# Two-layer hybrid block on one core: lookahead of three chunks in the mixer, the norm's gain on the activations, compression chunks spread through the weight stream

## The chip, the cores and the metric

One core of a Trainium2 chip runs the whole program. The metric is the device time of one execution in microseconds; three executions of the kernel before took 1166.40, 1166.65 and 1167.07 us, and the median, 1166.65 us, is what the change is measured against.

## What is computed

Two layers, each of a SwiGLU, a mixer and a second SwiGLU on 256 tokens of width 1024, each behind an RMS norm with a gain and added to the residual:

```python
for l in range(DEPTH):
    x = x + 0.5 * swiglu(rms_norm(x, norm_ffn1[l]), ffn1_wi[l], ffn1_wo[l])
    h = rms_norm(x, norm_mix[l])
    (u, q_raw, k_cmp, v_cmp, k_sel, v_sel, k_win, v_win,
     nsa_gate, gate_a, gate_b) = jnp.split(h @ w_in[l], SPLIT_POINTS, axis=-1)
    y_a = s5_branch(u, ...)                  # complex diagonal state space, 64 states for each of 32 groups
    y_b = nsa_branch(q_raw, k_cmp, ...) @ nsa_w_up[l]   # attention over compressed, selected and near keys
    merged = jax.nn.sigmoid(gate_a) * y_a + jax.nn.sigmoid(gate_b) * y_b
    x = x + merged @ w_out[l]
    x = x + 0.5 * swiglu(rms_norm(x, norm_ffn2[l]), ffn2_wi[l], ffn2_wo[l])
```

Compression takes the keys and values in blocks of 32 tokens through a 2048x128 matrix (`cmp_w1`), a GELU and a 128x64 matrix, once for keys and once for values.

## The kernel before

**Precision.** Each weight and each activation is split into a high part in fp32r (`whi`, `hh`) and the rest (`wlo`, `hl`), and a product is three matmuls, `mm3`: high by high (L381), high by low (L382), low by high (L383). ScalarE writes the high part and VectorE subtracts it for the low part. Weights arrive as chunks of 128x1024 (`raw`, 512 KB, four buffers) by DMA from SP's queue, in the order that `plan` writes down, and are split by `_split0`: a chunk with a norm's gain in pieces of one row block, with the gain multiplied in (L169 on ScalarE, L170 on VectorE), others in one piece (L349). `next` hands out a chunk and prepares `LA`=2 chunks ahead; there are four `whi` and four `wlo` buffers. Chunks of the compression (`cmp_w1`) are used unsplit, straight from `raw`, and hold a raw buffer until their products are done.

**Order.** A gemm (`gemm`) takes 256 tokens as two halves t0 and t1, each with a PSUM bank `gu` of which there are two, and runs `mm3` for each chunk of weights, t0 and t1 in turn. The bank is emptied by ScalarE (an evacuation), and the next gemm's first matmul of that half waits for it. Behind each chunk a background generator (`pull`) puts in a few steps of the state space branch (`s5_main`) and later of the attention. The framework fixes each engine's order when it builds the program; each engine then runs its instructions in that order, and a semaphore holds an instruction until its inputs and its buffer are there.

**The mixer** (`mix`) runs eight gemms over `w_in`, four chunks each: u (512 columns), KC (384), VS (408), Q (512), GA (2 x 512), GB (2 x 512). After u come the norm's sum of squares (`norms`, L363, tied behind the high part of the newest split), its evacuation (L1282) and a transposition on VectorE; then KC. After VS come the compression's four chunks with 16 products each (L550), and the small matrices; then Q, whose evacuation is L1049. GA and GB are evacuated by a tanh (L1322). The state space branch multiplies u into the state (L550), rotates (`rotate`, L933 to L941 on VectorE), scans (L890), rotates back, and then forms y from three products for each group, one of u and two of the rotated state (L907). The end of the SwiGLU ahead (`finish`) transposes the residual in pieces of 128x512 (L375) and splits them into `hh` and `hl` (L349).

## Time and profile before

| | |
|---|---|
| median of 3 executions | 1166.65 us |
| profiled execution | 1167.36 us |
| its span, first to last instruction | 1165.6 us |
| TensorE busy | 1153.3 us (99%) |
| VectorE busy | 827.1 us (71%) |
| ScalarE busy | 671.9 us (58%) |
| mean granted clock of TensorE | 0.997 |
| layer 0's mixer in the span | about 202 to 396 us |
| layer 1's mixer | about 780 to 972 us |

TensorE is the engine to look at: the others matter where it waits for them. Busy time of TensorE includes time at a lower clock, so the waits and the granted clock are read together.

### The profile page before, as it was taken

How to read it: one execution, taken by the hardware profiler on the slowest of the kernel's cores; microseconds unless marked ns; L12 is line 12 of the kernel's file. 1: busy time of each engine (PE TensorE's matmuls, PEld its weight loads, DVE VectorE, ACT ScalarE, POOL GpSimd, SP SyncE). 2: the span in 40 equal slices, each digit the busy share in tenths (PEclk: the TensorE clock that was granted, in tenths of full speed). 3: DMA queues.
4: the chain of work that ended last, by engine and by line, in shares of the span. 5: the costliest groups of instructions: out<-in, count | busy, mean ns of one | idle time of the engine just before them, and what ended most of it. 6: DMA issues, size and time to landing. Idle time of an engine off the chain costs nothing.

```text
span 1165.6 us, 17595 instructions
## 1 busy us (share of the span) xinstructions
PE 1153.3 (99%) x6148; PEld 939.7 (81%) x6148; DVE 827.1 (71%) x1578; ACT 671.9 (58%) x1176; POOL 96.0 (8%) x177
## 2 busy tenths in 40 slices
PE   9999999999999999999999999999999999999998
PEld 6888887877877888888888888788788778888886
DVE  5798597797776665555567986977987666655654
ACT  6755665646674565555566565555667646555552
POOL 3000000021032000000030000002112200000000
PEclk9999999999999999999999999999999999999999
DMA  8765646464443566665665555565654335766662
GB/s 239 232 193 166 186 144 209 124 204 141 155 118 106 174 206 191 187 183 185 192 181 184 181 179 169 157 178 158 200 162 145 109 110 170 227 184 185 191 183 88
DMA packets 150266, 200.40 MB, mean 172 GB/s; under 512 B 10145, under 2 KB 121025, under 8 KB 150177
## 3 DMA queue, kind: packets, MB, share of 16 engines
q1 hardware_dynamic: 148656, 196.93, 55.4%
q0 software_dynamic: 1136, 1.82, 0.8%
q8 instruction: 48, 0.79, 0.3%
q10 hardware_dynamic: 384, 0.52, 0.2%
q14 instruction: 42, 0.34, 0.1%
HBM read 198.18 MB, written 1.05 MB: 171 GB/s over the span
## 4 chain that ended last, share of the span: by engine, by line
PE 95%; DVE 3%; ACT 1%; issue 0%; POOL 0%; DVEq 0%; ACTq 0%; POOLq 0%
PE gu L381 20%; PE gu L383 20%; PE gu L382 20%; PE yb L382 4%; PE yb L383 4%; PE yb L381 4%; PE ya L383 4%; PE ya L381 4%; PE ya L382 4%; PE tr L496 2%; PE yb L1238 1%; PE yb L907 1%; PE tr L375 1%; PE tr L1227 1%; PE gu L448 1%; PE ya L1194 1%
## 5 line engine op out<-in xcount | busy, mean ns | idle before, releaser
L169 ACT ACTIVATE whi<-raw,gcol 128x512 fp32r<-128x512 f32 (+2 forms) x480 | 316.2, 710 | 197.8 <-PE gu L382 84.7
L170 DVE SCALAR_TENSOR_TENSOR wlo<-raw,gcol,whi 128x512 fp32r<-128x512 f32 (+2 forms) x480 | 335.6, 738 | 108.2 <-ACT whi L169 106.2
L381 PE MATMUL gu<-whi,hh 128*128 128x512 f32 (+2 forms) x944 | 373.5, 396 | 1.8 <-ACT r L1322 1.8
L383 PE MATMUL gu<-wlo,hh 128*128 128x512 f32 (+2 forms) x944 | 367.7, 393 | 0.0
L382 PE MATMUL gu<-whi,hl 128*128 128x512 f32 (+2 forms) x944 | 367.6, 389 | 0.0
L349 DVE TENSOR_TENSOR wlo<-raw,whi 128x1024 fp32r<-128x1024 f32 x128 | 156.5, 1225 | 120.0 <-ACT whi L349 117.2
L381 PEld LDWEIGHTS gu<-whi,hh 128*128 128x128 f32 x944 | 177.9, 188 | 36.3 <-ACT r L1322 2.6
L382 PEld LDWEIGHTS gu<-whi,hl 128*128 128x128 f32 x944 | 178.1, 189 | 34.8 <-issue 0.2
L383 PEld LDWEIGHTS gu<-wlo,hh 128*128 128x128 f32 x944 | 177.3, 188 | 34.8 <-issue 0.3
L349 ACT CAST whi<-raw 128x1024 fp32r<-128x1024 f32 x128 | 134.4, 1053 | 121.2 <-PE gu L382 102.4
L382 PE MATMUL yb<-whi,w1k 128*128 128x512 f32 x176 | 71.2, 406 | 0.2
L382 PE MATMUL ya<-whi,w1k 128*128 128x512 f32 x176 | 68.7, 392 | 0.0
L383 PE MATMUL yb<-wlo,w1k 128*128 128x512 f32 x176 | 68.1, 392 | 0.0
L381 PE MATMUL yb<-whi,w1k 128*128 128x512 f32 x176 | 68.0, 393 | 0.0
L381 PE MATMUL ya<-whi,w1k 128*128 128x512 f32 x176 | 67.6, 394 | 0.0
L383 PE MATMUL ya<-wlo,w1k 128*128 128x512 f32 x176 | 67.1, 390 | 0.0
L349 ACT CAST w1k<-tr 128x256 fp32r<-128x256 f32 x88 | 32.4, 368 | 43.5 <-PE tr L496 43.1
L513 DVE SCALAR_TENSOR_TENSOR w1k<-gu,rs,w1k 128x256 f32<-128x256 f32 x88 | 42.0, 479 | 16.8 <-ACT w1k L512 16.8
L512 ACT ACTIVATE w1k<-gu,rs 128x256 f32<-128x256 f32 x88 | 40.9, 467 | 18.4 <-PE gu L383 15.7
L356 POOL TENSOR_SCALAR rs<-ss 128x1 f32<-128x1 f32 (+3 forms) x22 | 6.8, 309 | 523.8 <-ACT w2k L363 472.3
L1217 POOL TENSOR_SCALAR w2k<-w2k,sm 128x128 f32<-128x128 f32 (+1 forms) x64 | 35.1, 568 | 103.8 <-DVE sm L1209 48.6
L349 DVE TENSOR_TENSOR w1k<-tr,w1k 128x256 fp32r<-128x256 f32 x88 | 36.6, 419 | 9.9 <-ACT w1k L349 9.8
(316 smaller groups left out, 1378.9 us busy)
## 6 DMA issues: line engine op xcount, KB each, us to landing
raw<-in_ffn_wi_dram SPq DMA_DIRECT2D x352, 256.0 KB, 3.3
raw<-in_ffn_wo_dram SPq DMA_DIRECT2D x88, 512.0 KB, 3.6
raw<-in_w_in_dram SPq DMA_DIRECT2D x48, 512.0 KB, 4.5
raw<-in_ssm_w_glu_dram SPq DMA_DIRECT2D x32, 256.0 KB, 3.0
raw<-in_w_out_dram SPq DMA_DIRECT2D x16, 512.0 KB, 3.7
raw<-in_cmp_w_dram SPq DMA_DIRECT2D x8, 512.0 KB, 4.9
raw<-in_nsa_w_up_dram SPq DMA_DIRECT2D x16, 256.0 KB, 4.0
raw<-in_w_in_dram SPq DMA_DIRECT2D x8, 408.0 KB, 4.2
```

Source lines behind the costliest of these rows:

```text
L169: k.hi_ins[i] = k.nc.scalar.activation(hi[:, s], r[:, s], AF.Copy, scale=c)
L170: k.lo_ins = k.nc.vector.scalar_tensor_tensor(lo[:, s], r[:, s], c, hi[:, s].bitcast(F32), op0=ALU.mult, op1=ALU.subtract)
L349: return k.nc.scalar.copy(hi, src), k.nc.vector.tensor_sub(lo, src, hi.bitcast(F32))
L375: m = k.nc.tensor.transpose(b[:, i], src[:, i * 128:(i + 1) * 128], k.id)
L381: mm(ps, a[0], b[0], start=first, stop=False)
L382: mm(ps, a[1], b[0], start=False, stop=False)
L383: return mm(ps, a[0], b[1], start=False, stop=last)
L448: last[2] = k.nc.tensor.matmul(ps[t], stat(kk, t)[a], W[i][b][:, cs[j]], start=kk == 0 and a + b == 0 and j == 0, stop=kk == nk - 1 and (a ...
L496: nc.tensor.transpose(b[:, i], act[t][:, i * 128:(i + 1) * 128], k.id)
L512: m = nc.scalar.activation(sg, ps[t][:, :256], AF.Silu, scale=r[t])
L513: nc.vector.scalar_tensor_tensor(a, ps[t][:, 256:], r[t], sg, op0=ALU.mult, op1=ALU.mult)
L1217: G.tensor_scalar(w[:, i], p[:, i], cf[:, j:j + 1], 0.0, op0=ALU.mult, op1=ALU.add)
```

## The change

- `plan`: the chunks of the compression no longer stand together between VS and Q; two stand behind VS's third and fourth chunk, two behind Q's first and second. `gemm` takes a list of functions (`behind`), one run behind each chunk; `compress` now does one chunk at a time, and its small matrices (`compress1`) come behind Q's third chunk.
- The gain of the mixer's norm is multiplied into the transposed activations (`transp4` with `g`, L390 and L391) instead of into the columns of `w_in`; chunks of `w_in` are then split in one piece (L357).
- Lookahead in the mixer, up to the chunks of `w_out`, is `LM`=3 instead of 2. The raw buffers stay four.
- `s5_main`: the products of u (`out`, L913) are issued ahead of those of the state, and the first half's bank is opened between the two rotations.
- Keys of the selected and near attention are written twice side by side by `normrope` and transposed as 128x128 blocks, four for each half instead of two, and split into `kT` in one piece of 128 partitions instead of four of 64.

```diff
+        k.la = opt['LA']
...
         if g is None:
-            k.split(r, hi, lo)
+            sh = [n for _, n in k.chunks[i][0].ap[1:]] if not isinstance(k.chunks[i][0], tuple) else [1024]
+            n = int(np.prod(sh))
+            k.hi_ins[i] = k.split(r[:, :n], hi[:, :n], lo[:, :n])[0]
...
-        k.prepare(k.opt['LA'] if la is None else la)
+        k.prepare(k.la if la is None else la)
...
-        def cols(l, c0, n=512):
+        def cols(l, c0, n=512, behind=()):
+
             for i in range(4):
-                k.add(ap(k.a['w_in'], l, i * 256, 2, c0, n), g=(2 + l, i * 2))
+                k.add(ap(k.a['w_in'], l, i * 256, 2, c0, n))
+                for v in behind[i:i + 1]:
+                    if v is not None:
+                        cmp(l, v)
+
+        def cmp(l, v):
+            w1 = A['cmp_w1']
+            k.add(bass.AP(tensor=w1.tensor, offset=w1.offset + (l * 4096 + v * 1024) * 128,
+                          ap=[[128, 128], [128 * 128, 8], [1, 128]]), split=False)
...
-            cols(l, C_VS, 408)
-            w1 = A['cmp_w1']
-            for kv in range(2):
-                for i in range(2):
-                    k.add(bass.AP(tensor=w1.tensor, offset=w1.offset + ((l * 2 + kv) * 2048 + i * 1024) * 128,
-                                  ap=[[128, 128], [128 * 128, 8], [1, 128]]), split=False)
-            for c0 in (C_Q, C_GA, C_GA + 512, C_GB, C_GB + 512):
+            cols(l, C_VS, 408, (None, None, 0, 1))
+            cols(l, C_Q, 512, (2, 3))
+            for c0 in (C_GA, C_GA + 512, C_GB, C_GB + 512):
...
-    def transp4(k, src, t, half):
...
-        return k.split(b, k.hh[:, s, q], k.hl_[:, s, q]) + (m,)
+        if g is None:
+            return k.split(b, k.hh[:, s, q], k.hl_[:, s, q]) + (m,)
+        for i in range(4):
+            j = half * 4 + i
+            c, hi = k.gcol[:, g * 8 + j:g * 8 + j + 1], k.hh[:, j, q]
+            f = k.nc.scalar.activation(hi, b[:, i], AF.Copy, scale=c)
+            d = k.nc.vector.scalar_tensor_tensor(k.hl_[:, j, q], b[:, i], c, hi.bitcast(F32), op0=ALU.mult,
+                                                 op1=ALU.subtract)
+        return f, d, m
...
+    def gemm(k, stat, nk, cols, order=None, per=2, la=None, behind=()):
...
             i0 += w
+            for f in behind[i0 - 1:i0]:
+                f()
...
+        B = []
+
+        def out(h, v, m, first, last):
+            for q in range(4):
+                for e in range(2):
+                    p = (2 * h + e) * 4 + q
+                    nc.tensor.matmul(B[h][e * 64:(e + 1) * 64, q], v[:, p], m[:, p], start=first and q == 0, stop=last,
+                                     skip_group_check=True)
+                yield 0.2
+
...
-        yt = None
         for h in range(2):
             yield from k.rotate(Sp, Z, P['cs'], P['sn'], slice(h * 8, h * 8 + 8), -1)
+            B.append(k.bank((128, 4, 128), 'yb'))
+            yield from out(h, U4, P['K'], True, False)
         yh, yl = r4(F32R), r4(F32R)
-
-        T = ((U4, P['K']), (Sp[0], P['C'][0]), (Sp[1], P['C'][1]))
         for h in range(2):
-            bk = k.bank((128, 4, 128), 'yb')
-            for q in range(4):
-                for i, (v, m) in enumerate(T):
-                    for e in range(2):
-                        p = (2 * h + e) * 4 + q
-                        nc.tensor.matmul(bk[e * 64:(e + 1) * 64, q], v[:, p], m[:, p], start=(q == 0 and i == 0),
-                                         stop=(i == 2), skip_group_check=True)
-                yield 0.6
+            bk = B[h]
+            for i in range(2):
+                yield from out(h, Sp[i], P['C'][i], False, i == 1)
...
-        V.tensor_add(out, tabs(t1), tabs(t2))
+        for o in out:
+            V.tensor_add(o, tabs(t1), tabs(t2))
...
-        kr = k.sb([128, 2, 2, 64], "w1k", k.opt['n1'])
+        kr = k.sb([128, 2, 2, 2, 64], "w2k", k.opt['n2'])
...
-        k.normrope(kp.rearrange("p b h d -> p (b h) d"), 4, cg, sg, kr, tb)
-        bk = k.bank((128, 2, 128))
-        for b in range(2):
-            nc.tensor.transpose(bk[:, b], kr[:, b].rearrange("p h d -> p (h d)"), k.id)
+        k.normrope(kp.rearrange("p b h d -> p (b h) d"), 4, cg, sg, [kr[:, :, :, e] for e in range(2)], tb)
+
+        bk = k.bank((128, 2, 2, 128))
+        for h in range(2):
+            for b in range(2):
+                nc.tensor.transpose(bk[:, h, b], kr[:, b, h].rearrange("p e d -> p (e d)"), k.id)
         q = slice(t * 128, (t + 1) * 128)
-        for h in range(2):
-            src = bk[h * 64:(h + 1) * 64]
-            for d in range(2):
-                o = slice(d * 64, (d + 1) * 64)
-                k.split(src, N['kT'][o, 0, h, :, q], N['kT'][o, 1, h, :, q])
+        k.split(bk, N['kT'][:, 0, :, :, q], N['kT'][:, 1, :, :, q])
...
+    def compress(k, kv, half):
+
+        nc, N = k.nc, k.N
+        if half == 0:
+            N['cp'] = k.bank((128, 33), 'ya')
+        ps, hid = N['cp'], N['hid']
+        w = k.next().rearrange("p (m c) -> p m c", m=8)
+        for m in range(8):
+            k.mm_cols(ps, [(w[:, m], N['kc2'][:, kv, m, half:half + 33])], half + m == 0, half * 8 + m == 15)
+        if half:
             pb = k.sb([128, 1], "pb", 2)
-            V.tensor_copy(pb, ps[:, 32:33])
-            S.activation(hid[:, kv, :, 0:15], ps[:, 0:32].rearrange("p (h n) -> p h n", h=2)[:, :, 0:15], AF.Gelu_apprx_tanh, bias=pb)
-
+            nc.vector.tensor_copy(pb, ps[:, 32:33])
...
+        k.la = k.opt['LM']
...
+        k.compress_in(kvT)
+        nop = lambda: None
+        ps = k.gemm(k.hstat, 8, 408, behind=(nop, nop, lambda: k.compress(0, 0), lambda: k.compress(0, 1)))
         for t in range(2):
             k.kv_evac(t, kp[t], ps[t])
-        cm = k.compress(kvT)
-        ps = k.gemm(k.hstat, 8, 512)
+        ps = k.gemm(k.hstat, 8, 512, behind=(lambda: k.compress(1, 0), lambda: k.compress(1, 1), k.compress1))
         N['qT'] = [k.sb([128, 4, 256], "qT", 2, F32R) for _ in range(2)]
         with k.tc.issue_after(k.mm.ins):
-            k.compress2(*cm)
+            k.compress2()
...
+        k.la = k.opt['LA']
...
-            k.ffn({6: h_nsa, 8: lambda: k.nsa_prep(l)}, 0.5, True, k.turns(k.opt['O2'] if l else k.opt['O1']))
+            k.ffn({6: h_nsa, 8: lambda: k.nsa_prep(l)}, 0.5, True, k.turns(k.opt['O2'] if l else k.opt['O1']), 2 + l)
...
-OPT = dict(nr=4, nh=4, LA=2, DLA=3, n1=10, n2=8, n4=7, n8=5, HP=2000, HN=2000, BG=1.2, FN=1, O1=22, WU=7, WV=7, SQ=1, LB=1, FB=2, O2=22, B1=1.0, B2=1.0)
+OPT = dict(nr=4, nh=4, LA=2, LM=3, DLA=3, n1=10, n2=8, n4=7, n8=5, HP=2000, HN=2000, BG=1.2, FN=1, O1=22, WU=7, WV=7, SQ=1, LB=1, FB=2, O2=22, B1=1.0, B2=1.0)
```

ScalarE at the passage from the SwiGLU to u and on to KC, layer 0. `hh` is the high part of the activations, `whi` of the weights (512 columns: u, 384: KC, 408: VS), `w2k,ss<-x` the squares of the norm, `w2k<-gu,rs` u's evacuation. Before:

```order
L349 CAST hh<-tr 128x4x128 x2
L169 ACTIVATE whi<-raw,gcol 128x512 x4
L349 CAST hh<-tr 128x4x128 x2
L169 ACTIVATE whi<-raw,gcol 128x384 x4
L363 ACTIVATE w2k,ss<-x 128x1024 x2
L1282 ACTIVATE w2k<-gu,rs 128x512
L169 ACTIVATE whi<-raw,gcol 128x384 x4
L1282 ACTIVATE w2k<-gu,rs 128x512
L169 ACTIVATE whi<-raw,gcol 128x408 x6
```

and after, where 768 columns are one whole chunk of KC and 816 one of VS:

```order
L390 ACTIVATE hh<-tr,gcol 128x128 x6
L357 CAST whi<-raw 128x1024 x2
L390 ACTIVATE hh<-tr,gcol 128x128 x7
L357 CAST whi<-raw 128x768
L390 ACTIVATE hh<-tr,gcol 128x128
L357 CAST whi<-raw 128x768
L390 ACTIVATE hh<-tr,gcol 128x128 x2
L357 CAST whi<-raw 128x768
L371 ACTIVATE w2k,ss<-x 128x1024 x2
L357 CAST whi<-raw 128x768
L1311 ACTIVATE w2k<-gu,rs 128x512 x2
L357 CAST whi<-raw 128x816 x3
```

Before, two of KC's four chunks are split ahead of the squares and u's first evacuation; after, three are split ahead of the squares and all four ahead of the evacuation, and the pieces of `hh` lie on both sides of u's and KC's splits.

TensorE at the end of VS and the start of Q (`ya<-kc,raw` is a compression product, `yb<-` a product of the state space branch, with r_1535 that of u, r_1614 and r_1615 those of the rotated state). Before:

```order
L381 MATMUL gu<-whi,hh 128x408
L382 MATMUL gu<-whi,hl 128x408
L383 MATMUL gu<-wlo,hh 128x408
L550 MATMUL ya<-kc_1851,raw 64x33 x64
L907 MATMUL yb<-r_1535,r_2320 64x128 x2
L907 MATMUL yb<-r_1614,r_2786 64x128 x2
L907 MATMUL yb<-r_1535,r_2320 64x128
L907 MATMUL yb<-r_1615,r_2787 64x128 x2
L907 MATMUL yb<-r_1535,r_2320 64x128
L381 MATMUL gu<-whi,hh 128x512
L382 MATMUL gu<-whi,hl 128x512
L381 MATMUL gu<-whi,hh 128x512
```

and after:

```order
L397 MATMUL gu<-whi,hh 128x408
L398 MATMUL gu<-whi,hl 128x408
L399 MATMUL gu<-wlo,hh 128x408
L568 MATMUL ya<-kc_1851,raw 64x33 x21
L397 MATMUL gu<-whi,hh 128x512
L398 MATMUL gu<-whi,hl 128x512
L399 MATMUL gu<-wlo,hh 128x512
L397 MATMUL gu<-whi,hh 128x512
L398 MATMUL gu<-whi,hl 128x512
L399 MATMUL gu<-wlo,hh 128x512
L568 MATMUL ya<-kc_1851,raw 64x33 x6
L397 MATMUL gu<-whi,hh 128x512
```

The 64 compression products stood in one row with state space products behind them; now 16 stand ahead of VS's last chunk (not shown), 21 ahead of Q's first, and the state space products have left this place.

TensorE around GA's first half (`tr<-id,w1k` transposes keys, `tr<-id,kb` and `tr<-cw,w1k` are the compression's small matrices). Before, the last products ahead of GA:

```order
L907 MATMUL yb<-r_1614,r_2786 64x128 x2
L907 MATMUL yb<-r_1615,r_2787 64x128 x2
L907 MATMUL yb<-r_1535,r_2320 64x128
L907 MATMUL yb<-r_1614,r_2786 64x128
L1035 MATMUL tr<-id,w1k 128x128 x2
L907 MATMUL yb<-r_1614,r_2786 64x128
L381 MATMUL gu<-whi,hh 128x512
L382 MATMUL gu<-whi,hl 128x512
L383 MATMUL gu<-wlo,hh 128x512
L381 MATMUL gu<-whi,hh 128x512
L382 MATMUL gu<-whi,hl 128x512
```

and after, in the middle of GA's first gemm, up to the first matmul of its second half:

```order
L913 MATMUL yb<-r_1535,r_2338 64x128
L913 MATMUL yb<-r_1614,r_2751 64x128 x2
L399 MATMUL gu<-wlo,hh 128x512
L397 MATMUL gu<-whi,hh 128x512
L398 MATMUL gu<-whi,hl 128x512
L399 MATMUL gu<-wlo,hh 128x512
L913 MATMUL yb<-r_1614,r_2751 64x128 x6
L913 MATMUL yb<-r_1615,r_2752 64x128 x4
L1141 MATMUL tr<-id,kb 128x32
L1148 MATMUL tr<-cw_1492,w1k 128x64
L913 MATMUL yb<-r_1615,r_2752 64x128 x4
L397 MATMUL gu<-whi,hh 128x512
```

The products of the rotated state stood before GA's first matmul, and GA ran on without them; now they stand behind GA's twentieth matmul and again between the two halves.

## Rows read from the trace of the kernel before

**Rows 1.** The page, the chain that ended last, share of the span by engine.

```profile
PE 95%; DVE 3%; ACT 1%; issue 0%; POOL 0%; DVEq 0%; ACTq 0%; POOLq 0%
```

**Rows 2.** TensorE's waits: line, what it waited for, us in total, times, longest.

```profile
PE yb L907 <- DVE r L936: 3.1, 2, 1.5
PE gu L381 <- ACT r L1322: 1.8, 2, 1.3
PE ya L300 <- POOL w1k L294: 1.4, 1, 1.4
```

**Rows 3.** Windows: PE, PEld, DVE, ACT, POOL busy, granted clock, DMA share, GB/s.

```profile
244.00:247.00 3.00, 1.46 (x39) 1.21 (x36) 3.00 (x8) 1.12 (x2) 0.85 (x2) 1.00 1.00 326
247.00:249.00 2.00, 1.87 (x12) 1.23 (x10) 1.74 (x5) 1.97 (x4) 1.15 (x1) 0.65 1.01 381
249.00:251.00 2.00, 2.00 (x12) 1.26 (x12) 2.00 (x7) 2.00 (x5) 0.00 (x0) 0.50 0.30 114
822.80:825.00 2.20, 0.65 (x11) 0.41 (x8) 2.20 (x7) 1.09 (x2) 0.82 (x2) 0.88 1.09 348
825.00:828.00 3.00, 3.00 (x16) 2.35 (x12) 2.74 (x8) 2.97 (x6) 1.16 (x1) 0.52 0.83 309
202.00:396.00 194.00, 190.28 (x1258) 156.02 (x1257) 143.52 (x258) 115.11 (x238) 33.43 (x61) 0.99 0.49 148
```

**Rows 4.** Timeline of TensorE: start, us, instruction, count [idle before <-releaser].

```profile
240.91 3.92 PE L550 MATMUL ya<-kc,raw 128*64 128x33 f32 x128
...
246.63 1.70 PE L907 MATMUL yb<-r,r 128*64 128x128 f32 x12 [1.54 <-DVE r L936]
```

**Rows 5.** Timeline of ScalarE, before GA's second column block.

```profile
272.75 5.50 ACT L169 ACTIVATE whi<-raw,gcol 128x512 fp32r<-128x512 f32 x8 [1.43 <-PE gu L382]
278.16 0.67 ACT L1322 ACTIVATE r<-gu,rh 128x512 f32<-128x512 f32 x1
```

**Rows 6.** Timeline of TensorE at the same place.

```profile
278.88 0.50 PE L381 MATMUL gu<-whi,hh 128*128 128x512 f32 x1 [1.27 <-ACT r L1322]
279.21 0.39 PE L382 MATMUL gu<-whi,hl 128*128 128x512 f32 x1
```

**Rows 7.** Timeline of ScalarE from u to KC, layer 0.

```profile
213.18 1.04 ACT L363 ACTIVATE w2k<-x 128x1024 bf16<-128x1024 f32 x1
...
214.22 1.04 ACT L363 ACTIVATE w2k<-x 128x1024 bf16<-128x1024 f32 x1
...
215.28 0.69 ACT L1282 ACTIVATE w2k<-gu,rs 128x512 f32<-128x512 f32 x1
216.32 1.12 ACT L169 ACTIVATE whi<-raw,gcol 128x384 fp32r<-128x384 f32 x2 [0.34 <-PE gu L382]
...
218.72 0.67 ACT L1282 ACTIVATE w2k<-gu,rs 128x512 f32<-128x512 f32 x1
```

**Rows 8.** Timeline of TensorE at the same place.

```profile
217.22 0.39 PE L382 MATMUL gu<-whi,hl 128*128 128x512 f32 x1
...
217.67 0.34 PE L381 MATMUL gu<-whi,hh 128*128 128x384 f32 x1
```

**Rows 9.** Timeline of ScalarE from u to KC, layer 1.

```profile
794.34 1.12 ACT L169 ACTIVATE whi<-raw,gcol 128x384 fp32r<-128x384 f32 x2 [0.34 <-PE gu L382]
```

**Rows 10.** Timeline of ScalarE ahead of u, layer 0.

```profile
205.06 2.56 ACT L169 ACTIVATE whi<-raw,gcol 128x512 fp32r<-128x512 f32 x4 [1.26 <-PE yb L382]
```

**Rows 11.** Timeline of TensorE in u, layer 0.

```profile
207.16 0.60 PE L375 MATMUL tr<-id,x 128*128 128x128 f32 x4
```

**Rows 12.** Groups by form, whole span: busy us, mean ns of one | idle before.

```profile
L349 ACT CAST whi<-raw 128x1024 fp32r<-128x1024 f32 x128 | 134.4, 1053 | 121.2 <-PE gu L382 102.4 <-issue 8.2 <-DMA raw<-in_ffn_wo_dram 3.9
...
L1167 ACT COPY pct<-tr 128x128 f32<-128x128 f32 x4 | 1.1, 265 | 1.1 <-PE tr L1165 1.1
```

**Rows 13.** The same view of 202 to 396 us.

```profile
L1146 DVE TENSOR_TENSOR cs<-cs,ss 128x128 f32<-128x128 f32 x2 | 0.6, 280 | 0.0
...
L1035 PE MATMUL tr<-id,w1k 128*128 128x128 f32 x4 | 0.8, 286 | 0.0
```

43 lines of the change are left out of this document (19 added, 24 removed).

## The prediction, made before the changed kernel ran

> **What bounds the kernel now.** I read four views. The chain that ended last is 95% TensorE [rows 1], so a time is won only where TensorE stands still or runs slowly. The list of TensorE's waits says how much that is: 3.1 us for the rotation L936 (two waits, one in each layer's mixer), 1.8 us for the tanh L1322 (two waits, both in layer 0), 1.4 us at the start of the program, which the change leaves alone [rows 2]. The windows show a second loss behind the first: TensorE is busy for 1.46 of 3 us at 244 to 247, and then the granted clock is 0.65 for 2 us and 0.50, the lower of its two levels (1.2 of 2.4 GHz), for 2 us more; in layer 1 it is 0.88 and 0.52 [rows 3]. ScalarE and VectorE are busy for 115 and 144 of the 194 us of layer 0's mixer [rows 3], so shorter splits there are worth nothing by themselves; only the order on these engines matters. Last I read the timelines around each of these places and around each place at which the change alters an order.
>
> **What the change removes.** (a) The rotation wait. Before, the four compression chunks' products run in one piece (128 short matmuls in 3.92 us), then the products L907 start, and after four of them TensorE stands for 1.54 us for the rotated state [rows 4]. After, the products are spread over the VS and Q gemms (order, second place), the products of u come from the middle of the Q gemm on, and those of the state start only 20 matmuls into GA0 (order, third place): the rotation has by then long run. Gone are 1.54 us and the slow clock behind it, 2 x 0.35 + 2 x 0.50 = 1.7 us, so 3.25 us; layer 1 gives 1.55 us of wait and 2.2 x 0.12 + 3 x 0.48 = 1.7 us of clock. Together 6.5 us. (b) The two waits for L1322, 0.55 and 1.27 us, in layer 0. The second is 1.27 us [rows 6] because the tanh stands behind eight pieces of split (5.50 us) on ScalarE and starts the moment they end [rows 5]. In the new order the tanh of GA0's first half has 14 products of the state and two small matmuls (order, third place) between its last product and the matmul that waits for its bank, some 2 us for 0.7 us of tanh; I count both waits as gone, 1.8 us. Removed in all: 8.3 us. The four raw buffers are no longer all held by compression chunks, so Q's weights are requested before the products end; in before their transfers collide (DMA share 1.01 at 244 to 247 [rows 3]). That matters only to Q's splits, and their wait is in (g).
>
> **What it adds.** (c) Three chunks ahead puts a third split ahead of an evacuation. This is the main term. Before, ScalarE does the two squares of the norm at 213.18 and 214.22, the evacuation L1282 of u's first half at 215.28, and only then KC's third split, at 216.32, when a matmul of u frees its buffer [rows 7]; KC's first matmul follows u's last at 217.67 without a gap [rows 8]. After (order, first place), the third split comes first, the squares behind it (they are tied to the newest split), then the fourth split, which waits for u's second-last matmul, and only then the evacuation, now L1311. KC's first matmul needs the bank that L1311 empties. Worked out from the rows: the third split cannot start before 216.32; a split of 128x768 takes three quarters of 1.053 us [rows 12], 0.8; the squares 2.1 (213.18 to 215.28); the fourth split 0.8; the evacuation 0.69. That is 220.7 against 217.67, so 3.05 us in which TensorE has nothing to do. Layer 1 has the same rows 578.02 us later [rows 9] and the same new order: 6.1 us. Bounds, from splits of 0.6 to 1.05 us: 2.6 to 3.5 each. Nothing else is queued on TensorE that could go ahead, as its next instructions belong to the same gemm; behind L1311 wait the transposition of u and all of the state space branch on VectorE, which shift with TensorE.
>
> (d) The clock behind (c). In before it fell behind 1.54 us without work that followed short matmuls, and did not fall behind 0.55 and 1.27 us between long ones: the two falls alone account for the mean of 0.99 over a mixer [rows 3]. A stop of 3 us between long matmuls does not occur in the trace. Bounds: nothing, or 1.7 us each as behind the rotation wait. The row nearest to it is the longer of the two, so I take 1.7 each, 3.4 us.
>
> (e) The gain now multiplies the transposed activations, in 128x128 pieces: 16 on ScalarE and 16 on VectorE for each layer instead of 4 and 4 of 128x512, where each piece on ScalarE waits for VectorE's piece of the same bank. Six pieces fit ahead of the two u splits at 205.06 [rows 10]; the last piece of the first bank comes behind them, at 207.0, and VectorE's behind that, at 207.3 to 207.6 (0.27 and 0.28 us of work each [rows 12, 13], and the hand over). The second half's transposition, which stood at 207.16 [rows 11], needs that bank: some 0.45 us later, 0.9 us for both layers (bounds 0 and 0.8 each). The row has no pieces of this kind, and "Perfetto Trace Analysis" of the Trainium skill ("Optimizing Scalar/DVE Operations") speaks the other way: where ScalarE or VectorE are not saturated but leave gaps on others, smaller instructions may let work end sooner. By that rule this term would be 0 and the sum 0.9 lower; no run so far shows it, and the order, with two splits between the pieces, is why I don't take it.
>
> (f) TensorE's own work: keys written twice are transposed by 8 matmuls for each layer instead of 4 (0.8 us busy for four [rows 13]; four transpositions in a row are 0.60 us with the tail of the last [rows 11]), so about 0.45; and the spread products make five more pairs of changes between the two number formats in the program, which cost the first long matmul behind one 0.1 us (0.33 us to the next at 278.88, against 0.225 at 217.22 [rows 6, 8]). 1.8 us for both layers, bounds 0.9 and 1.8. The key splits fall from 8 and 8 to 1 and 1 for each half; they lie beside Q and GA matmuls, and their cover was not exhausted: nothing gained.
>
> (g) Small waits. Q's second split now waits for a buffer that VectorE frees in the middle of the state's chain, and the evacuation of VS stands behind it on ScalarE; the key transpositions stand between the last compression products and need the norm of the keys. Both come out within 0.3 us of TensorE's arrival without (d), and behind it with (d). I take 0 with a slow clock, 0.6 us for both layers without; bounds 0 and 2 each. Chunk splits without the gain are one instruction of 1.05 instead of two of 0.67 us each: off the path, 0.
>
> **Sum.** -8.3 + 6.1 + 3.4 + 0.9 + 1.8 = +3.9 us. The profiled execution took 1167.36 us (span 1165.6), 0.7 above the median of 1166.65; the losses that I take from it should be the same in the median run, so the forecast is 1166.65 + 3.9 = 1170.5 us, slower by 0.33%.
>
> **Rivals.** One: the clock holds behind (c). For it: the stop comes straight behind long matmuls and ahead of long ones, and the shorter stops among such matmuls left the clock alone. Against it: 3 us is twice the stop that was followed by a fall. Then -8.3 + 6.1 + 0.9 + 1.8 + 0.6 = +1.1, 1167.8 us: no change. If it falls in one layer only, 1169.2.
> Two: faster. The evacuation is not held back, because ScalarE has room: KC's first matmul then starts as before, and -8.3 + 0.9 + 1.8 + 0.6 = -5.0 gives 1161.6 us. It decides where L1311 ends before u's last matmul, at 217.67. For it speaks only that ScalarE is idle for 40% of the mixer; against it that ScalarE has been seen to run an evacuation behind eight splits although its matmul had ended a microsecond earlier [rows 5]. Splits much shorter than 0.8 us would give a part of it.
> Three: slower still. With three splits ahead, every evacuation of GA and GB has one more split in front, and the bank of a gemm is needed as soon as the small matmuls between are over. If the tanh of GA1 and GB0 are late as L1322 was in before, 1.3 us each in both layers with (c) and (d), it is some 4 us more: 1174.5.
> Four: the change does not load further ahead: there are still four raw buffers, so "three ahead" moves splits and not transfers. That is how I read it, and it is in the sum.
>
> **How the numbers follow.** Forecast with a slow clock in both layers 0.35, in one 0.15, rival one 0.2, rival two 0.17, rival three 0.13. Within 0.2% (2.3 us, about what a measurement can tell from no change) lie 1164.3 to 1169.0: rival one mostly, half of the case of one layer, the near edges of the forecast and of rival two: 0.3. Faster: rival two and a little of one, 0.2. Slower: the rest, 0.5. The range of 1163 to 1174 leaves out most of rival two and the upper half of rival three.
>
> **What would show it.** In the profile after: a wait of KC's first matmul (gu, L397) for ScalarE's w2k, L1311, of about 3 us in each layer, first in the list of TensorE's waits; the granted clock behind it, 0.5 for some 3 us or 1.00; no wait for the rotation (L959, L964) and none for the tanh (L1352); the clock at 1.00 through the Q gemm; VectorE's pieces L391 interleaved with ScalarE's L390. I am wrong if L1311 of the first half ends before u's last matmul, if the largest new wait is another one, or if the Q gemm still starts at a slow clock.

## The result: slower by 0.8%, twice what was forecast

The changed kernel takes 1175.28 us (median of 4 runs, 1173.73 to 1176.64), the kernel before 1166.86 us beside it: a ratio of 1.0078, 95% interval 1.0066 to 1.009. The forecast was 1170.5 us, the range 1163 to 1174. The direction was right, the size was not: 8.4 us more instead of 3.9.

The profiled execution of after took 1176.23 us (span 1174.5, against 1165.6). TensorE is busy for 99% of it, and the chain that ended last is still 95% TensorE. The list of TensorE's waits, which answers to [rows 2], has changed entirely but for one line:

```profile
PE gu L397 <- ACT w2k L1311: 5.5, 2, 2.8
PE ya L308 <- POOL w1k L302: 1.4, 1, 1.4
PE tr L319 <- DMA w1k<-in_norm_ffn_dram: 1.0, 1, 1.0
PE tr L383 <- DVE hl L391: 0.9, 2, 0.5
```

The rotation and the tanh are gone from it. First stands KC's first matmul, which waits for the evacuation L1311, twice. (The third line is at the start of the program; no other kernel's trace has it.) ScalarE's timeline between u and KC in layer 0 answers to [rows 7]:

```profile
217.51 0.83 ACT L357 CAST whi<-raw 128x768 fp32r<-128x768 f32 x1 [0.48 <-PE gu L398]
218.25 1.05 ACT L371 ACTIVATE w2k<-x 128x1024 bf16<-128x1024 f32 x1
219.21 0.19 ACT L371 ACTIVATION_READ_ACCUMULATOR w2k<-x 128x1 f32 x1
219.30 1.04 ACT L371 ACTIVATE w2k<-x 128x1024 bf16<-128x1024 f32 x1
220.24 0.19 ACT L371 ACTIVATION_READ_ACCUMULATOR w2k<-x 128x1 f32 x1
220.34 0.81 ACT L357 CAST whi<-raw 128x768 fp32r<-128x768 f32 x1
221.06 1.25 ACT L1311 ACTIVATE w2k<-gu,rs 128x512 f32<-128x512 f32 x2
```

The third split, the two squares, the fourth split, and only then the evacuation: the order and the durations of the prediction. In layer 1 the clock falls behind the stop. TensorE's timeline there, and the windows of both layers (PE, PEld, DVE, ACT, POOL busy, granted clock, DMA share, GB/s):

```profile
798.01 0.40 PE L399 MATMUL gu<-wlo,hh 128*128 128x512 f32 x1
801.16 0.69 PE L397 MATMUL gu<-whi,hh 128*128 128x384 f32 x1 [2.75 <-ACT w2k L1311]
801.65 0.52 PE L398 MATMUL gu<-whi,hl 128*128 128x384 f32 x1
801.97 0.52 PE L399 MATMUL gu<-wlo,hh 128*128 128x384 f32 x1
```

```profile
222.00:225.00 3.00, 3.00 (x18) 3.00 (x18) 1.36 (x3) 0.31 (x1) 0.25 (x2) 1.00 0.36 109
...
801.00:804.00 3.00, 2.84 (x9) 2.84 (x10) 1.73 (x3) 0.68 (x2) 0.62 (x2) 0.50 0.36 117
804.00:807.00 3.00, 3.00 (x11) 3.00 (x10) 0.00 (x0) 0.00 (x0) 0.00 (x0) 0.50 0.35 104
807.00:810.00 3.00, 3.00 (x68) 2.75 (x69) 0.65 (x1) 0.00 (x0) 0.00 (x0) 0.95 0.02 5
```

In layer 1 a matmul of KC starts every 0.32 us and the granted clock is 0.50, the lower of its two levels, for some 6 us; in layer 0 it is 1.00 behind an equal stop. The fastest of the four runs, 1173.73 us, had a mean clock of 1.000, so even without any fall the change costs about 7 us against the median of before. That median has falls of its own; the runs of before at 1.000, beside the experiments, took 1164.9 to 1166.1 us, so at an equal clock the change costs some 8 us.

**Where the time went.** I cut both traces at the same instructions: from the transposition ahead of u to KC's first matmul, to VS's first, to the first matmul of the gate of the state space branch (L1361 in after), and to the end of the mixer. Worked out from the starts in TensorE's timelines, us:

| stretch | before, layer 0 | after, layer 0 | before, layer 1 | after, layer 1 |
|---|---|---|---|---|
| u, with the stop | 15.95 | 19.40 | 15.93 | 19.40 |
| KC | 12.46 | 12.45 | 12.46 | 15.25 |
| VS to GB | 90.36 | 90.13 | 89.00 | 90.13 |
| rest of the mixer | 74.53 | 72.58 | 73.11 | 72.59 |

u and KC are what was forecast: +6.9 us for the stop and the hand-off of pieces (forecast 7.0), +2.8 for the clock. The surprise is below. From VS on, 5.05 us in layer 0 and 3.25 in layer 1 of waits and slow clock should have gone, and 0.9 each come on top: -4.15 and -2.35. The table says -2.2 and +0.6. In the two layers 2.0 and 3.0 us are missing, 4.9 together, and the forecast missed by 4.8. None of the new waits in the list stands there. So TensorE works longer from VS on. A second reckoning agrees: TensorE's time from its first start to its last, less its gaps of over 0.2 us and less half of the time at a granted clock of 0.50 (the last microseconds of the program left out), is its own work. Worked out from the traces it is 1150.5 us before and 1156.9 after, 6.4 more. The experiments had to say at what.

### The profile page after: what moved, and what is told of

Same layout as the page of the kernel before. It is cut to its first block, busy times and chain, and to the rows that moved or that the text cites. A ratio compares the mean times of both kernels' runs of the same rounds, so it can differ in the third digit from the quotient of the medians.

```text
span 1174.5 us, 17498 instructions
## 1 busy us (share of the span) xinstructions
PE 1159.5 (99%) x6156; PEld 941.0 (80%) x6156; DVE 816.0 (69%) x1530; ACT 656.9 (56%) x1124; POOL 95.2 (8%) x177
## 3 DMA queue, kind: packets, MB, share of 16 engines
HBM read 198.18 MB, written 1.05 MB: 170 GB/s over the span
## 4 chain that ended last, share of the span: by engine, by line
PE 95%; DVE 2%; ACT 1%; issue 1%; POOL 0%; DMA 0%; SPq 0%; DVEq 0%; ACTq 0%; POOLq 0%
PE gu L397 20%; PE gu L399 20%; PE gu L398 20%; PE yb L398 4%; PE yb L399 4%; PE yb L397 4%; PE ya L399 4%; PE ya L397 4%; PE ya L398 4%; PE tr L514 2%; PE tr L383 1%; PE yb L913 1%; PE yb L1266 1%; PE ya L568 1%; PE gu L464 1%; PE tr L1255 1%
## 5 line engine op out<-in xcount | busy, mean ns | idle before, releaser
L357 DVE TENSOR_TENSOR wlo<-raw,whi 128x1024 fp32r<-128x1024 f32 (+2 forms) x192 | 229.8, 1202 | 144.4 <-ACT whi L357 141.4
L172 ACT ACTIVATE whi<-raw,gcol 128x512 fp32r<-128x512 f32 x352 | 234.1, 716 | 152.8 <-PE yb L398 69.0
L173 DVE SCALAR_TENSOR_TENSOR wlo<-raw,gcol,whi 128x512 fp32r<-128x512 f32 x352 | 249.3, 747 | 91.6 <-ACT whi L172 89.9
L357 ACT CAST whi<-raw 128x1024 fp32r<-128x1024 f32 (+2 forms) x192 | 198.3, 1036 | 188.5 <-PE gu L398 114.0
L357 ACT CAST w1k<-tr 128x256 fp32r<-128x256 f32 x88 | 32.4, 368 | 43.8 <-PE tr L514 43.5
L1245 POOL TENSOR_SCALAR w2k<-w2k,sm 128x128 f32<-128x128 f32 (+1 forms) x64 | 35.5, 573 | 120.4 <-DVE sm L1237 98.9
L357 DVE TENSOR_TENSOR w1k<-tr,w1k 128x256 fp32r<-128x256 f32 x88 | 36.6, 420 | 9.6 <-ACT w1k L357 9.3
```

Of the source, the lines that this page charges most:

```text
L172: k.hi_ins[i] = k.nc.scalar.activation(hi[:, s], r[:, s], AF.Copy, scale=c)
L173: k.lo_ins = k.nc.vector.scalar_tensor_tensor(lo[:, s], r[:, s], c, hi[:, s].bitcast(F32), op0=ALU.mult, op1=ALU.subtract)
L357: return k.nc.scalar.copy(hi, src), k.nc.vector.tensor_sub(lo, src, hi.bitcast(F32))
L1245: G.tensor_scalar(w[:, i], p[:, i], cf[:, j:j + 1], 0.0, op0=ALU.mult, op1=ALU.add)
```

## Experiments

Before the runs I held this theory: the stop at L1311 costs 5.5 us and at times the clock, and the rest is TensorE's own work, because the short products are cut into more pieces among the long ones. The rival was that a part of the change (spreading, the gain, the keys) does harm by a wait of its own. Ratios are to the kernel before, run beside each set, with 95% intervals; its medians there were 1166.0 to 1166.9 us.

### First set: one part of the change undone

**a_sq**: the squares tied to an earlier split.

```diff
-        with k.tc.issue_after(k.hi_ins[k.ns - k.opt['SQ']].ins):
+        with k.tc.issue_after(k.hi_ins[k.ns - k.opt['SQ'] - k.la + k.opt['LA']].ins):
```

> The changed kernel with one edit: in the mixer the norm's squares are tied to the second newest split instead of the newest, so that on ScalarE they and the evacuation L1311 of u's first half stand ahead of KC's third split again, with the lookahead still three. First theory (the evacuation behind the third and fourth split is the main cost, 2.75 us of waiting in each layer, and the slow clock follows from that stop): no wait for L1311, no slow clock behind u, so 5.5 us less and another 3 to 6 less by the clock: 1166 to 1169 us. Rival (TensorE's own work has grown by the many changes between long products and short ones, and the stop merely hides waits that come later): the wait for L1311 goes, but other waits of 1 to 2 us take its place and the time stays above 1171 us.

1170.14 us, ratio 1.0033 (1.002 to 1.0046). TensorE's waits, and the windows from u to KC in both layers:

```profile
PE ya L308 <- POOL w1k L302: 1.4, 1, 1.4
PE tr L383 <- DVE hl L391: 0.9, 2, 0.5
PE gu L464 <- ACT hh L357: 0.7, 1, 0.7
```

```profile
216.00:222.00 6.00, 6.00 (x33) 5.38 (x31) 2.78 (x6) 3.26 (x7) 1.73 (x6) 1.00 0.82 265
794.00:804.00 10.00, 10.00 (x53) 8.98 (x53) 5.28 (x8) 5.39 (x9) 1.72 (x6) 1.00 0.64 208
```

One edited line takes away the stop, the fall of the clock and 5.1 us. The time lies between the two expectations: the stop and the fall went as the first theory said, no new wait came as the rival had it, but the time stayed high as the rival had it. No wait that was not there before is left but 0.9 us for the pieces, the clock is 1.00, and still the kernel is 3.65 us slower than before, although 8.3 us of stops should have left it faster. The loss from VS on is therefore no echo of the stop. The edit also changed the order of the short products: the own work of a_sq is 1160.9 us, 4.0 more than that of the full change, so the 5.1 us are what was won less that.

**a_one**: the compression in one piece, ahead of the Q gemm.

```diff
-            cols(l, C_VS, 408, (None, None, 0, 1))
-            cols(l, C_Q, 512, (2, 3))
+            cols(l, C_VS, 408)
+            for v in range(4):
+                cmp(l, v)
+            cols(l, C_Q, 512)
...
```

> The changed kernel with the compression's four chunks in one piece between VS and Q again (weights and products), all else as changed. First theory (each change between long and short products costs about 0.3 us, and spreading makes some six more of them in each layer): TensorE's intervals around the short products shrink by 1.5 us in each layer, 3 us less in all: 1172.3 us, with the 2.75 us waits for L1311 unchanged. Rival (spreading is what keeps the clock up and hides the rotation, its changes are cheap): the one piece of short products brings a slow clock or a wait at the start of Q back, 1 to 2 us in each layer, and the time is 1175 to 1178 us.

1178.1 us, ratio 1.0104 (1.0089 to 1.0119): slower than the full change by 2.8. TensorE's waits:

```profile
PE gu L399 <- ACT w2k L1313: 5.5, 2, 2.8
...
PE tr L1063 <- DVE w2k L1041: 1.3, 2, 0.7
PE gu L399 <- ACT whi L359: 1.3, 2, 0.7
PE gu L401 <- DVE wlo L359: 1.2, 1, 1.2
```

In one piece, the four compression chunks starve the split of the next weights and leave the norm of the keys without cover, 3.8 us of new waits. The granted clock is also at 0.50 for 3.4 us at the start of Q in layer 0 (from 253.8 us), where it is 1.00 in the full change; the rival came true. The spreading buys something.

**a_key1**: the keys written once, 4 transpositions for each layer instead of 8.

```diff
-        for h in range(2):
-            for b in range(2):
-                nc.tensor.transpose(bk[:, h, b], kr[:, b, h].rearrange("p e d -> p (e d)"), k.id)
+        for b in range(2):
+            nc.tensor.transpose(bk[:, b], kr[:, b].rearrange("p h d -> p (h d)"), k.id)
...
```

> The changed kernel with the keys written and transposed once again (two transpositions for each half, and eight 64-partition splits on ScalarE and on VectorE), all else as changed. First theory (transpositions are TensorE's own work): four fewer transpositions in each layer, 0.45 to 1.3 us less each, so 1172.7 to 1174.4 us. Rival (the sixteen small splits alternate between ScalarE and VectorE on one bank for some 7 us and hold back evacuations): waits for the key splits or the evacuation of Q appear, and the time is 1175 us or more.

1171.65 us, ratio 1.0047 (1.0032 to 1.0061), 3.6 below the full change, with the stop at the evacuation as before (5.5 us). I had priced the four transpositions at 0.9 us for both layers. Four transpositions cannot take 1.8 us for each layer, so something else went with them. In the profiled executions 1.7 us of it are clock (at 0.50 for 3.4 us behind the stop of layer 1, against 6.7 in the full change) and 2.2 us are own work (1154.7 against 1156.9); the second set was to say what.

**a_gainw**: the gain on w_in again.

```diff
-                k.add(ap(k.a['w_in'], l, i * 256, 2, c0, n))
+                k.add(ap(k.a['w_in'], l, i * 256, 2, c0, n), g=(2 + l, i * 2))
...
```

> The changed kernel with the norm's gain multiplied into the columns of w_in again (two pieces for each split) and the transposed activations split in pieces of 128x512, all else as changed. First theory: the 0.45 us wait of the second half's transposition for VectorE goes in both layers, 0.9 us less, but each split ahead of L1311 is two pieces of 0.6 us instead of one of 0.8, so that its wait grows from 2.75 to 3.3 us or more: between 1174.5 and 1176 us, no difference beyond the spread of the runs. Rival (the shorter splits of the changed kernel are worth something elsewhere, since ScalarE stands ahead of many evacuations): waits for evacuations appear in GA and GB and the time is 1178 us or more.

1175.73 us, ratio 1.0081 (1.0065 to 1.0096), no different from the full change. The wait for the pieces (L391, 0.9 us) is gone, and the stop has grown from 5.5 to 6.6, as splits with the gain are two instructions each. The two cancel.

### Second set: is it the number of breaks?

**a_sq_key1** (a_sq and a_key1 together), **a_sq_coarse** and **a_sq_key1_coarse** (the products with the state's matrices handed on 32 at a time):

```diff
-                                     skip_group_check=True)
-                yield 0.2
+                                     skip_group_check=True)
+            yield 0.8
```

> The changed kernel with two edits: the squares of the norm tied to the second newest split (as in a_sq, 1170.1 us), and the keys written once and transposed by 4 matmuls for each layer (as in a_key1). First theory: what is left of the loss in a_sq is TensorE's own work, above all the number of places at which short products break into the long ones (220 in the program of a_sq, 212 in this one, 206 before) and the four transpositions more; the two edits then add up: 1170.1 less the 3.6 us that a_key1 gained on the changed kernel = 1166.5 us, level with before. Rival: a_key1 gained by a lucky order only, the keys cost nothing: 1169 to 1171 us.

> a_sq with one edit: the products with the state's matrices are handed to the stream 32 at a time and not 8 at a time. The instructions are the same, but the order that results breaks the long products at 236 places instead of 220. First theory: such a break costs TensorE about 0.4 us (0.66 + 1.55 + 0.77 + 0.61 us for some nine breaks more in layer 1, a_sq against before), so 16 more cost 6 us: 1170.1 + 6 = 1176 us, without any new wait of over 1 us. Rival: breaks are free, since TensorE does the same work in another order: 1170 us. If a new wait of over 1 us for another engine shows up, the run says nothing on breaks.

> a_sq_key1 with the products of the state handed on 32 at a time: here the order has 200 breaks against 212 of a_sq_key1, the same instructions otherwise. First theory (0.4 us for a break): 4.8 us below a_sq_key1, so some 1162 us, below the kernel before. Rival (breaks are free): the time of a_sq_key1, 1166 to 1170 us.

Measured, ratios beside the same runs of before: a_sq_key1 1164.24 us (0.9979, 0.9969 to 0.9989), a_sq_coarse 1168.38 (1.0016, 1.0006 to 1.0025), a_sq_key1_coarse 1166.68 (1.0, 0.9991 to 1.0009). a_sq_key1 gained more than the first theory said. The other two refute its price: 16 more breaks made the kernel 1.8 us faster than a_sq, 12 fewer made it 2.4 slower than a_sq_key1. The second of these has a new wait of 2.0 us for the tanh (L1355) that accounts for most of it; the first has none of over 0.2.

The rows show what a break is made of. TensorE's timeline of after, around the first pieces of the compression in VS:

```profile
242.60 0.35 PE L398 MATMUL gu<-whi,hl 128*128 128x408 f32 x1
242.78 0.34 PE L399 MATMUL gu<-wlo,hh 128*128 128x408 f32 x1
243.06 1.12 PE L568 MATMUL ya<-kc,raw 128*64 128x33 f32 x32
244.11 0.46 PE L397 MATMUL gu<-whi,hh 128*128 128x408 f32 x1
244.41 0.35 PE L398 MATMUL gu<-whi,hl 128*128 128x408 f32 x1
...
246.26 0.34 PE L399 MATMUL gu<-wlo,hh 128*128 128x408 f32 x1
246.53 1.47 PE L568 MATMUL ya<-kc,raw 128*64 128x33 f32 x42
247.93 0.50 PE L397 MATMUL gu<-whi,hh 128*128 128x512 f32 x1
```

Long matmuls of 408 columns start every 0.185 us. The step into the piece is 0.28 (243.06 - 242.78), so 0.095 too much; its 32 records (16 products, two records each) at 0.03 are 0.95, and the piece takes 1.05, so 0.1 on the way out; the first long matmul behind it holds the next back by 0.30 instead of 0.185, another 0.115. That is 0.31 us for one place, whatever is in it. I had taken 0.1. All products on 64 columns of the stationary, the operand that a weight load puts into TensorE ahead of the matmul (128*64 in the rows: compression, u into the state, products of the state, values), show these steps, those of the state with 0.14 on the way out, 0.35 together. Transpositions and the products of the keys, 128*128, show no step on the way in. Counted in the order of TensorE's instructions, a group of 128*64 products of one kind ends at 42 places in before (two of them straight into the next group) and at 60 in after; 64 in a_sq, 58 in a_sq_coarse, 54 in a_sq_key1 and in a_sq_key1_coarse, and a_key1. (The expectations below give 2 to 6 more for each kernel, as I had counted the few products of the compressed values with them, which are 128*128.) So a_sq_coarse has more breaks than a_sq, but 6 fewer of the dear kind, and a_sq_key1_coarse, with fewer breaks, has no fewer of these.

**b_u**: the kernel before with the products of u ahead and nothing else (the other four parts undone).

> The kernel before with one part of the change alone: the products of u ahead of those of the state, everything else as before (two chunks ahead, gain on the weights, compression in one piece, keys once); 208 breaks against 206. First theory: the rotation wait of 1.5 us in each layer and the slow clock behind it (1.3 to 1.7 us) go, one break more in each layer costs 0.4, the L1322 waits stay: 1166.5 - 6.2 + 0.8 = 1161 us. Rival: the products that stood behind the rotation now leave the compression's norm or the tanh without cover, and the wait only changes its name: 1165 to 1167 us, with a wait of over 1 us for VectorE or ScalarE in the Q or GA0 gemm.

1163.89 us, ratio 0.9976 (0.9967 to 0.9985): faster, but by 3 and not by 5.5. Both expectations are half right: the rotation and the tanh are out of the list, and a new wait, for the split of a weight chunk, has taken half of the gain. TensorE's waits:

```profile
PE gu L399 <- ACT whi L172: 3.0, 2, 1.6
PE ya L310 <- POOL w1k L304: 1.4, 1, 1.4
PE gu L466 <- ACT hh L359: 0.7, 1, 0.7
```

### Third set: fewer places

With a_sq_key1 as the base: **a_sq_key1_pair** (compression in two places of two chunks), **a_sq_key1_one** (in one), **a_sq_key1_gainw** (gain on the weights); and **b_u_spread** (before, with products of u ahead and the compression spread).

```diff
-            cols(l, C_VS, 408, (None, None, 0, 1))
-            cols(l, C_Q, 512, (2, 3))
+            cols(l, C_VS, 408, (None, None, None, (0, 1)))
+            cols(l, C_Q, 512, (None, (2, 3)))
...
```

> a_sq_key1 (1164.2 us) with the compression's products in two places of two chunks for each layer and not four of one. The traces of the second set put a price on each kind of short product: float32 products (compression, products of the state, values) cost 0.095 us going in, 0.15 to 0.20 coming out and 0.11 on the first long matmul, 0.35 us net for a place; transpositions and the products of kT cost 0.1 to 0.2. The count of all breaks, my price before, was the wrong measure; the places where a float32 group ends count (44 in before, 64 in the changed kernel, 68 in a_sq, 62 in a_sq_coarse, 56 in a_sq_key1). Here they are 50. New theory: 6 x 0.35 = 2.1 us less, 1162.1 us. Rival (places of float32 products cost nothing, a_sq_key1 gained by its transpositions alone): 1164.2 us. A new wait of over 1 us would make the run tell nothing.

> a_sq_key1 with the compression in one piece: 8 places of the compression fewer, but the rest of the order shifts and the products of the state get 5 and the values 4 places more, so float32 groups end at 57 places against 56. New theory: the time of a_sq_key1, 1164.5 us. Rival (what costs is the spreading of the compression itself): 8 x 0.35 = 2.8 us less, 1161.4 us. Second rival (spreading covers the norm of the keys and the weights, as in a_one, 2.8 us slower than the changed kernel): 1167 us, with a wait of over 1 us.

> Two parts of the change on the kernel before: the products of u ahead and the compression spread; two chunks ahead, gain on the weights, keys once. Float32 groups end at 50 places against 48 in b_u (1163.9 us), +0.7; in b_u the compression in one piece left TensorE waiting 3.0 us for the split of a weight chunk behind it, which should go when the four chunks no longer come in a row. New theory: 1163.9 + 0.7 - 3.0 = 1161.6 us. Rival (the wait moves to another place): 1164 us or more.

> a_sq_key1 with the gain on the weights again. TensorE's instructions are then in the same order as in b_u_spread, so the two differ only by three chunks ahead (with the squares tied to the second newest split) against two. 50 places against 56 in a_sq_key1: -2.1 us, and the wait for the last piece with the gain (0.9 us) goes: 1161.2 us. Theory: three chunks ahead is worth nothing by itself, so within 0.7 us of b_u_spread. Rival: the third chunk covers a late weight, then over 1 us below b_u_spread.

| kernel | places | us | ratio to before | TensorE's waits that a_sq_key1 lacks, over 1 us in sum |
|---|---|---|---|---|
| a_sq_key1_gainw | 48 | 1163.0 | 0.9972 (0.996 to 0.9983) | none |
| b_u_spread | 48 | 1164.07 | 0.9981 (0.9972 to 0.9991) | none (three of 0.5 to 0.9) |
| a_sq_key1_pair | 48 | 1166.47 | 1.0006 (0.9998 to 1.0015) | keys' norm 2.8, L357 1.4 |
| a_sq_key1_one | 53 | 1171.12 | 1.0041 (1.0028 to 1.0054) | split 2.5, keys' norm 1.3 |

The pair ran into the norm of the keys (TensorE's waits of that kernel):

```profile
PE tr L1060 <- DVE w1k L1039: 2.8, 2, 1.4
PE ya L308 <- POOL w1k L302: 1.4, 1, 1.4
PE gu L397 <- ACT r L357: 1.4, 2, 0.7
```

By its own condition it tells nothing of places (less these 4.2 us it would stand at 1162.3, where the theory had it). In one piece the second rival came true, by 4 us more than it said: the clock fell too (mean 0.996). a_sq_key1_gainw is the fastest kernel of the study, 3.5 us faster than before. It and b_u_spread run the same order on TensorE, so three chunks ahead against two is worth 1.1 us at most by the medians, and the intervals overlap. The difference is the clock: five of b_u_spread's twelve runs had a mean clock of 0.997 or 0.998 and took 1165.3 to 1168.1 us, and the median of the other seven is 1162.9, level with a_sq_key1_gainw (0.999 and 1.000 in all six). So at an equal clock three ahead shows no gain, as the theory had it; that the medians lie 1.07 us apart, as its rival asked, is the clock. b_u_spread itself was expected at 1161.6 us and missed that; its trace has small waits and none of over 1 us but the one at the start of the program. Over the kernels of these sets with the squares moved and without a new wait of over 1 us the time rises with the places: 48, 54, 58, 64 places and 1163.0, 1164.2, 1168.4, 1170.1 us, 0.44 us each, though the last two hold four transpositions more for each layer, and the four do not lie on a line. The own work, which leaves waits and the clock out, says the same over more kernels: 1150.5 us in before (42 places), 1150.3 in b_u (46), 1151.8 to 1152.4 in the three of the table with 48, 1154.1 in a_sq_key1_one (53), 1154.4 to 1155.2 in the three with 54, 1156.6 in a_gainw (56), 1158.3 in a_sq_coarse (58), 1156.9 in the full change (60), 1160.9 in a_sq (64); a_one, with 48 and the keys twice, has 1155.3. At 0.33 us for a place and 0.9 for the keys' second transpositions each comes out within 2.2 us. So what grows is work and not waits, but the count does not give each kernel to the microsecond.

### Fourth set: the price of a place by itself

The order could not be held still by leaving things out, so I added: 48 places of products that nobody reads, in the last six gemms of each mixer, whose matmuls were chained in the order in which they are written (control **c_0**). One product of 128x128 by 33 columns (**c_f1**), four (**c_f4**), one transposition (**c_t1**), then one and four products of 128x64 (**c_h1**, **c_h4**).

```diff
+                if kk in (1, 3):
+                    f += [lambda: nc.tensor.matmul(k.dum[:, 0:33], k.id, k.id[:, 0:33], start=True, stop=True)] * 1
...
```

> Control for the three kernels beside it: a_sq_key1_gainw (1163.0 us) with the matmuls of the last six gemms of each layer's mixer (the gate of the state space branch and the projection of the attention) held in the order in which they are written, and one bank set aside. Nothing is added. Both theories: 1163 to 1166 us, as the held order may open small waits.

> c_0 with 48 float32 products of 33 columns added that nobody reads, two for each row block of each of the last six gemms of a mixer, each alone between long products (40 of 48; 8 stand beside other short work). Theory: a place costs what the rows of the earlier traces say, 0.095 going in, 0.153 until the next long product starts and 0.109 on that one, 0.36 us; 40 x 0.36 + 8 x 0.2 = 16 us over c_0. Rival: a place costs what I took in the prediction, 0.1 us and the product's own 0.03: 6 us over c_0.

> c_f1 with four products in each place instead of one, 192 in all. Theory: what costs is the place and not the product; three more cost 3 x 0.03 = 0.09 us in each, 4.3 us over c_f1, 20 us over c_0. Rival: the cost goes with the products, four times that of c_f1.

> c_0 with 48 transpositions of 128x128 in the same places instead of the float32 products. Theory: the kind matters; a transposition costs 0.01 to 0.06 going in, 0.05 until the next long product and 0.09 on that one, 0.15 to 0.2 us; 40 x 0.17 + 8 x 0.12 = 8 us over c_0, half of c_f1. Rival: every break of the long products costs the same whatever breaks it, as in my second set's expectations: the time of c_f1.

> c_f1 (1180.0 us) with the added products on half of the stationary's columns, 128x64 as in the compression and in the products of the state, and not 128x128. In c_f1 the first long product behind a place costs 0.09 and the way out 0.10, but the way in cost nothing (0.00 against 0.095 us before the compression's products), so a place came to 0.2 and not to 0.36. Theory: it is the narrower tile, 64 columns among tiles of 128, that makes the difference, 0.095 going in, 0.15 out, 0.11 on the next: 0.36 against 0.21 in c_f1, 44 x 0.15 = 6.5 us more, 1186.5 us. Rival: it is the float32 format alone, half of the columns are half of the work: 1178 to 1180 us.

> c_h1 with four products in each place, 192 in all. In c_f4 three more products of 128x128 cost 0.2 us each, where the compression's 128x64 come every 0.03 us in the rows. Theory: with the narrow tile the place costs and the product hardly: 144 x 0.03 = 4.3 us over c_h1. Rival: these lone products cost 0.2 us each as in c_f4: 28 us over c_h1.

| kernel | us (ratio to before) | over c_0 | for each of 48 places | the same from own work |
|---|---|---|---|---|
| c_0 | 1172.84 (1.0034 to 1.0074) | | | |
| c_t1 | 1175.39 (1.0062 to 1.0102) | 2.6 | 0.05 | 0.10 |
| c_f1 | 1180.03 (1.0101 to 1.014) | 7.2 | 0.15 | 0.23 |
| c_h1 | 1189.09 (1.0173 to 1.0213) | 16.3 | 0.34 | 0.44 |
| c_h4 | 1205.35 (1.0313 to 1.0354) | 32.5 | 0.68 | 0.79 |
| c_f4 | 1208.36 (1.0345 to 1.0386) | 35.5 | 0.74 | 0.87 |

The control was dearer than expected, in part because the held order made waits of its own. Waits of 5.3 us are in c_0 and in none of the others, others (1.3 to 4.0 us, for VectorE at L1385) are only in the five, and c_0's trace alone has a stretch at a granted clock of 0.50 (955.4 to 958.8 us, 1.7 us lost). So the differences to c_0 are some microseconds too small. The last column leaves waits and clock out (own work 1155.6 us in c_0, 1160.6, 1166.6, 1176.5, 1193.5 and 1197.1 in the order of the table). One place in c_t1, c_f1 and c_h1 each, in TensorE's timelines:

```profile
350.82 0.39 PE L449 MATMUL gu<-wlo,r 128*128 128x512 f32 x1
351.05 0.27 PE L448 MATMUL yb<-id 128*128 128x128 f32 x1
351.08 0.71 PE L449 MATMUL gu<-whi,r 128*128 128x512 f32 x2
```

```profile
352.07 0.40 PE L449 MATMUL gu<-wlo,r 128*128 128x512 f32 x1
352.30 0.30 PE L448 MATMUL yb<-id 128*128 128x33 f32 x2
352.44 0.71 PE L449 MATMUL gu<-whi,r 128*128 128x512 f32 x2
```

```profile
348.84 0.40 PE L449 MATMUL gu<-wlo,r 128*128 128x512 f32 x1
349.17 0.30 PE L448 MATMUL yb<-id 128*64 128x33 f32 x2
349.40 0.73 PE L449 MATMUL gu<-whi,r 128*128 128x512 f32 x2
```

The long products start every 0.23 us. Into a transposition, and into a product of 128*128, the step is 0.23: nothing. Into a product of 128*64 it is 0.33, 0.1 more. To the next long product it is 0.03, 0.14 and 0.23. Two long products then take 0.71, 0.71 and 0.73 instead of 0.62 (as at 353.01 in c_h4 below). So a place with one product costs 0.12, 0.23 and 0.44 us, which is what the own work says. My second set's rival (every break costs the same) is out, and so is "the float32 format": the narrower stationary is what costs most, with half of the columns; why it does, no run here shows. c_h1 came out above its expectation, by 2.6 us; c_f1 at less than half of it, since I had taken the narrow price for a wide product; c_t1 at a third, as its places cost 0.12 and not 0.15 to 0.2 and the control's waits and clock hide a part.

The other half of the theory, that the products in a place cost next to nothing, did not hold for these: 144 more cost 28.3 us in c_f4 and 16.3 in c_h4, 0.2 and 0.11 each; c_h4's rival, 28 us, failed too. In the rows a product leaves two records, so the 0.03 of the compression are for half a product; I had read them as a whole one. TensorE's timeline of c_h4:

```profile
353.01 0.62 PE L449 MATMUL gu<-whi,r 128*128 128x512 f32 x2
353.47 0.39 PE L449 MATMUL gu<-wlo,r 128*128 128x512 f32 x1
353.79 0.65 PE L448 MATMUL yb<-id 128*64 128x33 f32 x8
354.37 0.73 PE L449 MATMUL gu<-whi,r 128*128 128x512 f32 x2
```

Three products more lengthen the way to the next long product from 0.23 to 0.58 us: 0.06 us for each record, against 0.03 within the compression. Why these are dearer I did not try; they all write the same spot, which those of the compression do within a chunk, too.

## Why the prediction was off, step by step

- **(a), (b): the waits removed.** Right. Neither the rotation nor the tanh is in any list of after, and the clock is 1.00 in both layers from VS on. Of the 8.3 us, nothing shows a shortfall that could be told from (f).
- **(c): the evacuation behind the third and fourth split.** Right in place, order and size: 2.75 us in each layer against 3.05. That the wait is real, and removable, a_sq shows.
- **(d): the slow clock behind it.** 3.4 us were taken, 1.7 in each layer. In the profiled execution it fell in layer 1 alone and cost 2.8 there; in the fastest run not at all. The right sum, nearly, by luck: the fall here lasted longer than the one behind the rotation wait, and it doesn't come each time. In a_key1 it came in layer 1 and in a_gainw, behind stops of 3.3 us, in both, for 3.4 us each time, which is 1.7 us as taken. One reading was wrong: the stops of 0.55 and 1.27 us that left the clock alone came behind two small matmuls each (270.43 and 277.17 us), not straight between long ones.
- **(e): the hand-off of pieces.** 0.9 us forecast, 0.9 in the list of waits. I set this term against "Perfetto Trace Analysis" of the Trainium skill ("Optimizing Scalar/DVE Operations"), by which smaller instructions on an unsaturated engine may let work end sooner. Here the trace disagrees with it: TensorE waits for the last piece 0.9 us longer, and with the gain back on the weights (a_gainw) that wait is gone.
- **(f): TensorE's own work. This is the step that failed.** It stood at 1.8 us for both layers and measured 1.8 + 4.9 = 6.7 (6.4 by the own work). Two things were wrong in it. The price: "the first long matmul behind one 0.1 us" counted one of three steps, from a row (278.88) that stands behind transpositions and a wait; the way into a group of 128*64 products and the way out of it cost about 0.1 us each as well, 0.31 to 0.35 us together in the rows, without the products, and c_h1's 0.34 over c_0, or 0.44 of own work, holds one product. And the count: "five more pairs of changes in the program" are five in each layer for the compression alone (six groups instead of one, so ten in the program); at five in all, 0.9 + 5 x 0.1 would be 1.4 and not 1.8. The state's products, handed on in more and smaller lots (with u ahead, 24 lots in each layer instead of 8), gave nine more groups (20 instead of 11), and the values one fewer, so that 18 places came to be added. 18 x 0.31 to 0.35 is 5.6 to 6.3 us; with the transpositions themselves, 0.9, that is 6.5 to 7.2, and 6.7 was measured. That this agrees so closely is in part luck, as the other kernels miss the same sum by up to 2.2 us. The count could have been had before the run from the order; the prediction took three places of it and not the sum.
- **(g): small waits.** None above 0.3 us inside the mixers: 0, as taken.
- **The rivals.** That the clock holds was true of some layers and runs, and would have been +1.1 + 4.9 with the right (f): 1172.7 us, near the fastest run of 1173.73. "Faster" failed at L1311 as foreseen. "Slower still" gave nearly the right time by the wrong mechanism: no tanh is late. "Three ahead moves splits and not transfers" stands: in layer 0's mixer SP issues the same chunks in the same order from 200.92 to 243.46 us in a_sq_key1_gainw (three ahead) and from 201.37 to 243.91 in b_u_spread (two); it costs the order at L1311 and shows no gain.

Undone one at a time, the parts of the change come out as: products of u ahead, worth 3.0 us alone; the spreading, nothing that shows beside that alone (2.4 us together), but 2.8 in the full change; the gain, nothing either way here; the keys twice, 3.6 us lost in the full change and 5.9 without the stop, through the order more than through the transpositions; three ahead, 5.1 us lost to the squares' tie, net of four places more, and nothing won at an equal clock. What remains when the losing parts go is 1163.0 us.
